# SwiGLU_1's opening in staircase order, its first two modulation columns on TensorE, and the mixer's first projection ahead of its norm

## The chip, the core and the metric

The kernel runs on one core of a Trainium2 chip. The metric is the device time of one execution in microseconds (us): the median of the timed runs. Engines are named as in the profile: PE is TensorE (matmuls), PEld its weight loads, DVE VectorE, ACT ScalarE, POOL GpSimd and SP SyncE, which issues most DMAs.

## The reference

One decoder layer of a batch of one: T = 256 tokens, model width D = 2048, feed-forward width FF = 5632, all in float32.

```
x = x + 1/2 * gate1 * SwiGLU_1(mod(norm(x)))          # shift 0, scale 1, gate 2 of nine adaLN vectors
x = x + gate2 * W_out [ FoX(heads 0..7) || GatedDeltaNet(heads 0..7) ](mod(norm(x)))   # shift 3, scale 4, gate 5
x = x + 1/2 * gate3 * SwiGLU_2(mod(norm(x)))          # shift 6, scale 7, gate 8
out = norm(x)

mod(norm(x)) = x * rsqrt(mean(x*x) + eps) * g * (1 + scale) + shift
swiglu(h)    = (silu(h @ wg) * (h @ wu)) @ wd
nine vectors = silu(c) @ ada_w + ada_b                # ada_w: 2048 x 18432, 144 columns of 128 outputs
```

The mixer has one input projection. It gives queries, keys and values of 8 forgetting-attention heads (FoX: softmax attention whose logits take a cumulated log forget gate) and of 8 gated-delta-net heads (a causal convolution of 4 taps, silu, L2 norm, and a recurrence over chunks of 64), besides small gates.

## The kernel before

**Layout.** Features lie on the 128 partitions, so x is 16 slices (`x[:, j]`, `KD` = 16) of 128 features x 256 tokens. All large products are exact to float32 by a split: an operand is a rounded high half plus a low remainder, and each 128x128 tile of a weight takes three matmuls, high x high, high x low and low x high (`three`, `mm`, `products`; matmuls into `pgu`, `pd`, `pp`).

**The weight stream.** `W` (class `Stream`) hands out weight tiles in the order in which the program asks for them. 8 tiles are a block of 512 KB, 674 blocks in all. `W.block(b)` issues the DMA to `wraw` on SP and the cast to the high half `whi` on ACT (L123); `W.next` adds the remainder `wlo` = `wraw` - `whi` on DVE (L135). FFN 1 takes blocks 0 to 263: 112 for the first 28 of 44 feed-forward slices of gate and up (`gate_up_first`), 56 for their down projection, 64 for gate and up of the other 16 slices, 32 for their down projection. The mixer starts at block 264.

**The adaLN columns.** Each of the 144 columns is 1 MB, and DVE reduces it against silu(c) in one instruction (L260, `adat` or `adaf`). `RATE` lists from which block on how many columns are handed out for each block (`W.side`). `ada_need` says that a column must be there before what follows. SwiGLU_1 needs 32 of them (shift 0 and scale 1, in turns by j) before its 16 slices of normalized input.

**The start.** ACT sums the squares of x and takes silu of c, which four one-row matmuls spread over the partitions (`pcs`, L658); PE turns x into features by 32 transposes (`px`, L679) and the reciprocal norm into a row (`nrow`, L709); DVE takes the first two columns in halves (`first_col`, L694). Warm-up matmuls on zeros (`zp`, L201) stand at two places (`N_WARM`).

**The first half of SwiGLU_1.** For slice j of the input, `modulate_one` makes `ht` on DVE (L368), the high half of `hs` on ACT, and the low half on DVE (L372 for odd j, L376 for even j). `gate_up_first` covers the inner dimension k in chunks 0 to 2, 2 to 8 and 8 to 16 (`CHUNKS`). In each chunk the 28 slices go in groups of 8, 8, 8 and 4; the first group goes k by k for the first 2, 5 and 5 values (`LEAD`), everything else slice by slice. Partial sums go to `acc`: 28 copies on ACT after the first chunk, 28 additions on DVE after the second, and the last chunk closes with silu and product.

**The norms.** A norm needs the sum of squares (`nsum`), its reciprocal root, and that as a row (`nrow`). Before the mixer, `modulate(1, 3, 4)` does all this, and then the first projection starts, slice by slice as `hs` is made (L769 to L771). For SwiGLU_2, the class `Early` does it another way: the first products are of x times the gain, ahead of the norm; the row then multiplies the result, and the shift is added through two more columns of the moving operand (`scaled`).

**The mixer.** Its steps are Python generators. Each `yield` states how much PE time should pass until its next part; the list `ORDER` says which heads come when. The keys' squared norms need a transposing matmul (`pkk`, L937) and an evacuation on ACT; `decays` is a run of logarithms and exponentials on ACT (L905). A FoX head has the places `plog` (logits), `ppt` (transposed weights, L1167), `pfo` (output), `pft` (transposed output, L1189).

**Order on an engine.** The program's order is not the order of issue: a list scheduler puts each engine's instructions in a fixed order when the kernel is built, and `tc.issue_after` and `tc.keep_in_program_order` bind it. At run time each engine goes through its own list in order.

Of the kernel before, what the change touches and what calls it, by code (L numbers as in the profile page):

```python
# [16 lines left out]
P = 128  # L17
D = 2048
# [5 lines left out]
CHUNKS = (0, 2, 8, 16)  # L24
LEAD = (2, 5, 5)
# [8 lines left out]
RATE = ((0, 0.5), (24, 0.34), (56, 0.45), (68, 0.06), (112, 0.5), (168, 0.38), (264, 0.0), (284, 0.26), (404, 0.0), (424, 0.125))  # L34
# [3 lines left out]
N_WARM = (10, 7)  # L38
# [3 lines left out]
LATER = 8  # L42
BEHIND = 2
# [47 lines left out]
class Stream:  # L91


    def __init__(self, nc, w, raw, hi, lo):
        self.nc, self.w, self.raw, self.hi, self.lo = nc, w, raw, hi, lo
        self.order = []
        self.more = None
        self.h = self.l = self.last = None
        self.owed, self.side, self.quiet = 0.0, lambda: None, False
        self.tc, self.hold, self.held = None, None, []  # L100
        self.first = []
        self.late, self.owing = False, []

    def settle(self, upto=N_TILES):

        while self.owing and self.owing[0][0] <= upto:
            self.owing.pop(0)[1]()

    def behind(self, later=True):
# [3 lines left out]
        return nullcontext() if self.hold is None else self.tc.issue_after(self.hold)  # L113

    def block(self, b):
# [7 lines left out]
        self.cast = self.nc.scalar.copy(self.h, r).ins  # L123
        return r, lo

    def next(self, mat, k, n, width=1):
        i = len(self.order)
        if i % WB == 0:
# [5 lines left out]
            with self.behind():  # L134
                lo_ = nc.vector.tensor_tensor(self.l, r, self.h.bitcast(F32), ALU.subtract)  # L135
            with self.tc.issue_after(lo_.ins):
                self.settle(b - BEHIND)
# [12 lines left out]
def layer_kernel(ctx: ExitStack, tc: tile.TileContext, xrow, c, adaw, cols, cst, w, out, order, dbg=None):  # L150
# [86 lines left out]
    def ada_col():  # L237
# [26 lines left out]
        if W.late:  # L264
            W.owing.append((len(W.order) // WB, total))
# [3 lines left out]
    def ada_need(m, j):  # L269
# [3 lines left out]
        W.settle()  # L273
# [81 lines left out]
    plain = hsf[:, : KD * HS].rearrange("p (k i) -> p k i", k=KD)[:, :, : 2 * T].rearrange("p k (q t) -> p k q t", q=2)  # L355

# [7 lines left out]
    def modulate_one(j, g1, sh, r, weave=True):  # L364

        t = pt("ht")
        hl, hh, tt = (run(j, LO), run(j, HI), turns(t)) if weave else (plain[:, j, LO], plain[:, j, HI], t)
        V.scalar_tensor_tensor(t, x[:, j], g1, r, ALU.mult, ALU.mult)  # L368
        if j % 2:
# [3 lines left out]
        else:  # L373
            with tc.issue_after(W.cast) if W.first else nullcontext():
                A.activation(hh, tt, AF.Identity, bias=sh)  # L375
# [9 lines left out]
    def modulate(which, m_sh, m_sc):  # L385
        ada_need(max(m_sh, m_sc), KD - 1)
        g1 = gains(which, m_sc, 0, KD)
        r = norm_row(norm_sums())
        hq["next"], hq["one"] = 0, lambda j: modulate_one(
            j, g1[:, j : j + 1], mod[:, m_sh * KD + j : m_sh * KD + j + 1], r, False)  # L390

    class Early:
# [3 lines left out]
        def __init__(self, which, m_sh, m_sc):  # L396
            self.which, self.m_sh, self.m_sc, self.row, self.rstd = which, m_sh, m_sc, None, None

        def y(self, j):
# [8 lines left out]
            A.activation(run(j, HI), turns(x[:, j]), AF.Copy, scale=g)  # L408
            V.scalar_tensor_tensor(run(j, LO), turns(x[:, j]), g, run(j, HI).bitcast(F32), ALU.mult, ALU.subtract)  # L409

        def step(self, k):
# [3 lines left out]
            if k == 4:  # L415
# [3 lines left out]
                    j, g1[:, j : j + 1], mod[:, self.m_sh * KD + j : self.m_sh * KD + j + 1], self.row)  # L419
# [8 lines left out]
        def scaled(self, dst, ps):  # L428
# [4 lines left out]
            V.tensor_tensor(dst, ps[:, :T], self.row, ALU.mult)  # L433
# [118 lines left out]
    def gate_up_first(fs, hp):  # L552
# [5 lines left out]
        groups = [fs[i : i + 8] for i in range(0, len(fs), 8)]  # L558
        chunks = list(zip(CHUNKS[:-1], CHUNKS[1:]))
# [17 lines left out]
        def evacuate(ps, f, ci):  # L577
            if ci == 0:
                acc[f] = hp.tile([P, 2 * T], F32, name="acc", tag="hid")
                A.copy(acc[f], ps)  # L580
            elif ci < len(chunks) - 1:
# [7 lines left out]
        for ci, (k0, k1) in enumerate(chunks):  # L589
            for gi, grp in enumerate(groups):  # L590
                if gi == 0 and LEAD[ci]:
                    pb = {f: bank() for f in grp}
                    ks = k0 + LEAD[ci]
                    for k in range(k0, ks):
                        ada_need(0, k)
                        for f in grp:
                            for s in range(2):
                                three(pb[f], f, s, k, k0, k1)
                    for f in grp:
                        for k in range(ks, k1):  # L600
                            ada_need(0, k)
                            for s in range(2):
                                three(pb[f], f, s, k, k0, k1)
                        evacuate(pb[f], f, ci)
                else:
                    for f in grp:
                        pf = bank()
                        for k in range(k0, k1):
                            ada_need(0, k)
                            for s in range(2):  # L610
                                three(pf, f, s, k, k0, k1)
                        evacuate(pf, f, ci)
        return hids

    def ffn(which, m_gt, early=None):
        fs = list(range(NF))
        with tc.tile_pool(name=f"hid{which}", bufs=PARTS[which][1] + HIDX) as hp, \
                tc.tile_pool(name=f"more{which}", bufs=1) as more:
            W.more = more if MORE else None
            for half in range(2):  # L620
# [7 lines left out]
                def after(j):  # L628
                    residual(pds.pop(j), j, m_gt, True)
                    if half == 1:  # L630
                        sumsq_add(j)
                        if which == 1:
# [22 lines left out]
    pcs = []  # L655
    for q in range(4):
        pcs.append(psn(q + 1, "pcs"))
        PE.matmul(pcs[q], one[:1], crow[:, q * 512 : (q + 1) * 512], start=True, stop=True)  # L658

# [6 lines left out]
    for kind, i in (("x", 0), ("x", 1), ("c", 0), ("c", 1), ("x", 2), ("x", 3), ("c", 2), ("c", 3)):  # L666
        with nullcontext() if hold is None else tc.issue_after(hold):
            if kind == "c":
                hold = cond(i)
            else:  # L670
# [4 lines left out]
    def features(i):  # L675
        px = psn(i, "px")
# [6 lines left out]
    for i in range(4):  # L683
        features(i)
# [760 lines left out]
```

## Time and profile before

| | |
|---|---|
| median of 3 runs | 1943.49 us (1943.44 to 1944.72) |
| profiled execution, own time | 1943.79 us |
| its span | 1941.9 us, from the first to the last instruction |
| mean granted TensorE clock | 0.992 |
| PE busy | 1903.0 us, 98% of the span |
| PEld, DVE, ACT, POOL busy | 1777.2, 1554.0, 1041.2, 56.8 us |
| first matmul into `pgu` | 22.52 us |
| FFN 1, mixer, FFN 2 with the last norm | to about 741 us, to about 1238 us, to the end |

Shares are of the whole span. PE busy at 98% says little about where time can be had: a stage in which PE waits, or in which its clock is granted at half, shows only in views of that stage. Busy PE time also counts matmuls that run at half the clock.

### The profile page before, as it was taken

The numbers are of one execution on the slowest core, as the hardware profiler recorded it, in microseconds if no ns is written. First come the engines' busy times: TensorE is split into PE (matmuls) and PEld (weight loads), VectorE is DVE, ScalarE is ACT, GpSimd is POOL, SyncE is SP. The second block draws the span as 40 slices with busy tenths as digits, with TensorE's granted clock in tenths as the row PEclk, the third lists the DMA queues.
The fourth block names the chain that finished last, engine by engine and source line by source line (L and its number), as shares of the span: only waits on it lengthen the run. The fifth ranks groups of instructions, "written<-read, shape, count | busy, mean of one in ns | idle before, by whom it ended". The sixth has DMA issues, their size and how long they took to land. (4 is left out here: it accounts for less than half of the span.)

```text
span 1941.9 us, 33701 instructions
## 1 busy us (share of the span) xinstructions
PE 1903.0 (98%) x13087; PEld 1777.2 (92%) x13087; DVE 1554.0 (80%) x2415; ACT 1041.2 (54%) x1647; POOL 56.8 (3%) x55
## 2 busy tenths in 40 slices
PE   8999999999999999999999999999999999999998
PEld 6999999998999988889989998999999999999997
DVE  6999978989989997779987989976777665666654
ACT  6544555433455446858657655665554445555553
POOL 0000000000000030000000001100000000000011
PEclk8999999999999999999999999999999999999999
DMA  9989867999999975586667568667767665565663
GB/s 371 359 308 358 305 224 258 400 369 376 356 358 339 361 302 212 212 314 220 214 242 257 201 218 303 208 258 252 245 253 257 244 225 200 201 200 202 202 200 120
DMA packets 129490, 519.58 MB, mean 268 GB/s; under 512 B 18217, under 2 KB 21545, under 8 KB 111153
## 3 DMA queue, kind: packets, MB, share of 16 engines
q1 hardware_dynamic: 129330, 517.42, 72.9%
q8 instruction: 103, 1.69, 0.3%
q14 instruction: 57, 0.47, 0.1%
HBM read 512.89 MB, written 4.47 MB: 266 GB/s over the span
## 5 line engine op out<-in xcount | busy, mean ns | idle before, releaser
L135 DVE TENSOR_TENSOR wlo<-wraw,whi 128x1024 fp32r<-128x1024 f32 x674 | 822.3, 1226 | 268.3 <-ACT whi L123 267.3
L123 ACT CAST whi<-wraw 128x1024 fp32r<-128x1024 f32 x674 | 700.6, 1047 | 515.1 <-PE pd L485 166.5
L485 PE MATMUL pd<-hid,whi 128*128 128x512 f32 x1408 | 461.8, 382 | 0.0
L486 PE MATMUL pd<-hid,wlo 128*128 128x256 f32 x1408 | 384.6, 273 | 2.6 <-DVE wlo L135 2.6
L260 DVE CUSTOM_DVE_ANT_0 adat<-adat,cs,colt 128x2048 f32<-128x2048 f32 x140 | 329.2, 2351 | 6.5 <-DMA adat<-in_ada_dram 6.5
L481 PE MATMUL pg<-hs,whi 128*128 128x512 f32 x912 | 302.2, 382 | 0.5 <-DVE shc L432 0.5
L481 PE MATMUL pu<-hs,whi 128*128 128x512 f32 x912 | 302.2, 382 | 0.0
L485 PEld LDWEIGHTS pd<-hid,whi 128*128 128x128 f32 x1408 | 266.0, 189 | 36.9
L486 PEld LDWEIGHTS pd<-hid,wlo 128*128 128x128 f32 x1408 | 270.3, 192 | 5.4 <-DVE wlo L135 5.3
L567 PE MATMUL pgu<-hs,whi 128*128 128x256 f32 x896 | 245.8, 277 | 5.9 <-ACT hs L371 5.9
L482 PE MATMUL pu<-hs,wlo 128*128 128x256 f32 x912 | 249.2, 273 | 0.0
L482 PE MATMUL pg<-hs,wlo 128*128 128x256 f32 x912 | 248.9, 273 | 0.0
L569 PE MATMUL pgu<-hs,wlo 128*128 128x256 f32 x896 | 245.1, 278 | 2.4 <-DVE wlo L135 2.4
L568 PE MATMUL pgu<-hs,whi 128*128 128x256 f32 x896 | 246.5, 277 | 0.0
L481 PEld LDWEIGHTS pg<-hs,whi 128*128 128x128 f32 x912 | 172.4, 189 | 24.8 <-ACT shc L431 0.7
L481 PEld LDWEIGHTS pu<-hs,whi 128*128 128x128 f32 x912 | 172.4, 189 | 23.6
L769 PE MATMUL pp<-hs,whi 128*128 128x256 f32 x656 | 188.9, 289 | 1.6 <-ACT hs L375 1.6
L770 PE MATMUL pp<-hs,whi 128*128 128x256 f32 x656 | 182.9, 279 | 0.0
L771 PE MATMUL pp<-hs,wlo 128*128 128x256 f32 x656 | 182.7, 278 | 0.0
L567 PEld LDWEIGHTS pgu<-hs,whi 128*128 128x128 f32 x896 | 172.9, 194 | 6.7 <-ACT hs L371 6.3
L482 PEld LDWEIGHTS pu<-hs,wlo 128*128 128x128 f32 x912 | 175.0, 192 | 1.0 <-DVE wlo L135 0.9
L482 PEld LDWEIGHTS pg<-hs,wlo 128*128 128x128 f32 x912 | 175.1, 192 | 0.4
(337 smaller groups left out, 2593.8 us busy)
## 6 DMA issues: line engine op xcount, KB each, us to landing
wraw<-in_w_dram SPq DMA_DIRECT2D x674, 512.0 KB, 4.4
adat<-in_ada_dram SPq DMA_DIRECT2D x140, 1024.0 KB, 7.2
xr<-in_xr_dram SPq DMA_DIRECT2D x4, 512.0 KB, 5.3
adaf<-in_ada_dram SPq DMA_DIRECT2D x4, 512.0 KB, 8.5
adaf<-in_ada_dram SPq DMA_DIRECT2D x2, 1024.0 KB, 12.3
xd<-x SPq DMA_DIRECT2D x4, 512.0 KB, 7.0
rw<-rowd SPq DMA_DIRECT2D x16, 128.0 KB, 4.3
x<-xd SPq DMA_DIRECT2D x4, 512.0 KB, 5.8
```

What stands on the lines that cost most here:

```text
L123: self.cast = self.nc.scalar.copy(self.h, r).ins
L135: lo_ = nc.vector.tensor_tensor(self.l, r, self.h.bitcast(F32), ALU.subtract)
L260: V.tensor_tensor_reduce(t, t, cs, 1.0, L("adab", q, 1), ALU.mult, ALU.add, mod[:, q : q + 1])
L481: PE.matmul(ps, wt[0], both, start=(k == 0), stop=False)
L482: PE.matmul(ps[:, T:], wt[1], part(k, HI), start=False, stop=(k == KD - 1))
L485: PE.matmul(ps, wt[0], act.rearrange("p q (a b) -> p q b a", a=2), start=first, stop=False)
L486: PE.matmul(ps[:, :T], wt[1], woven(act[:, 0]), start=False, stop=last)
L567: PE.matmul(o, wh, part(k, HI), start=first and s == 0, stop=False, skip_group_check=skip)
L568: PE.matmul(o, wh, part(k, LO), start=False, stop=False, skip_group_check=skip)
L569: PE.matmul(o, wl, part(k, HI), start=False, stop=last, skip_group_check=skip)
L769: PE.matmul(pp[i][:, :T], wh, hh, start=(k == 0), stop=False)
L770: PE.matmul(pp[i][:, :T], wh, hl, start=False, stop=False)
```

## The change

1. **Staircase.** In `gate_up_first` the table `PIECES` (group, first k, k by k up to, last k) takes the place of `CHUNKS` and `LEAD`. The four groups take turns at the low k, so that a slice of the input is used by many matmuls before the next is asked for. Evacuations are put off in a list `owed`. There are 28 copies on ACT as before; of additions on DVE there are 32 in the place of 28. The sums of the columns are finished behind the next block's `wlo` from the start (`W.late`).
2. **First two columns on PE.** silu(c) is also made as columns (`pct`: 16 one-column matmuls; `csk`), and the first two adaLN columns are 16 matmuls each of one column (`pcol`, L717 of the changed kernel), whose weights the host has packed for it. `px` uses three PSUM buffers of one pool. Half of the `pcs` matmuls come later. Block 0 is cast and subtracted in two halves. Warm-up matmuls: 10, 2 and 2 in the place of 10 and 7.
3. **First projection of the mixer ahead of its norm.** `Early` serves here too (`norm1`); `modulate` and the layout `plain` go. The gates and three key heads are scaled by the row and shifted afterwards.
4. **Residuals later.** In the feed-forward parts the residual of one output slice is placed at step 18 (at most the last but one) of the next slice, before at step 8.
5. **RATE.** The pace of the columns is retuned.
6. **Spacing.** FoX steps ask for 1.5, 4.5, 1.5 and 6.5 in the place of 1, 3, 1 and 5; `decays` for 3 in the place of 1.

The diff, cut:

```diff
-CHUNKS = (0, 2, 8, 16)
-LEAD = (2, 5, 5)
+PIECES = (
+    (0, 0, 1, 1), (1, 0, 1, 1), (2, 0, 2, 2), (3, 0, 3, 3), (0, 1, 4, 4), (1, 1, 6, 6), (3, 3, 7, 7),
+    (2, 2, 11, 11), (3, 7, 12, 12), (0, 4, 11, 16), (1, 6, 6, 16), (2, 11, 11, 16), (3, 12, 12, 16),
+)
-RATE = ((0, 0.5), (24, 0.34), (56, 0.45), (68, 0.06), (112, 0.5), (168, 0.38), (264, 0.0), (284, 0.26), (404, 0.0), (424, 0.125))
+RATE = ((0, 0.5), (12, 0.45), (68, 0.06), (112, 0.5), (168, 0.42), (232, 0.24), (264, 0.0), (288, 0.27), (404, 0.0), (424, 0.125))
-N_WARM = (10, 7)
+N_WARM = (10, 2, 2)
-LATER = 8
+LATER = (18, 8)
...
+        owed = []
+        for g, k0, ks, k1 in PIECES:
+            grp = fs[8 * g : 8 * g + 8]
+            pb = {}
...
+            for k in range(k0, ks):
+                for f in grp:
+                    both(f, k)
+            for f in grp:
+                for k in range(max(k0, ks), k1):
+                    both(f, k)
+                owed.append(lambda f=f, ps=pb[f], k0=k0, k1=k1: evacuate(ps, f, k0, k1))
+                while ks < k1 and len(owed) > 1:
+                    owed.pop(0)()
...
+    pct = psf("pct")
+    for k in range(KD):
+        PE.matmul(pct[:, k : k + 1], crow[:, k * P : (k + 1) * P], one[:1, :1], start=True, stop=True)
...
+    def first_col(i):
+        m, j = ada_seq[i]
+        q = m * KD + j
+        for k in range(KD):
+            PE.matmul(pcol[:, i : i + 1], first_ada[i][:, k * P : (k + 1) * P], csk[:, k : k + 1], start=(k == 0),
+                      stop=(k == KD - 1), skip_group_check=True)
+        return V.tensor_tensor(mod[:, q : q + 1], pcol[:, i : i + 1], L("adab", q, 1), ALU.add)
...
-        modulate(1, 3, 4)
...
-        first = project([("gt", 0)] + [("qkv", NH + h) for h in range(3)])
+        W.lag = 2
+        first = project([("gt", 0)] + [("qkv", NH + h) for h in range(3)], norm1)
...
-                        if j and q == LATER:
+                        if j and q == min(LATER[0], len(part) - 2):
                             after(j - 1)
...
-            yield 3.0
+            yield 4.5
             ppt = psf("ppt")
```

PE's own order at the start, from the warm-up matmuls to the first product of SwiGLU_1 (`pgu`). Before:

```order
L201 MATMUL zp<-zw 128x512
L658 MATMUL pcs<-crow,one 128x512 x4
L679 MATMUL px<-colt,xr 128x128 x24
L709 MATMUL nrow<-colt,frb 128x128 x2
L679 MATMUL px<-colt,xr 128x128 x8
L201 LDWEIGHTS zw
```

and in the changed kernel:

```order
L676 MATMUL pcs<-crow,one 128x512 x2
L682 MATMUL pct<-one,crow 128x1 x16
L706 MATMUL px<-colt,xr 128x128 x12
L717 MATMUL pcol<-csk,adaf_118 128x1 x3
L706 MATMUL px<-colt,xr 128x128 x8
L717 MATMUL pcol<-csk,adaf_118 128x1 x5
L706 MATMUL px<-colt,xr 128x128 x5
L717 MATMUL pcol<-csk,adaf_118 128x1 x8
L733 MATMUL nrow<-colt,frb 128x128 x2
L706 MATMUL px<-colt,xr 128x128 x7
L676 MATMUL pcs<-crow,one 128x512 x2
```

Behind these stand two warm-up matmuls, 16 of L717 for the second column, two more warm-up matmuls and the first `pgu`. So 48 one-column matmuls have come into PE's queue ahead of it, and 3 of 17 warm-up matmuls have gone.

DVE's own order at the same place, from the first low half of `hs` on (`adaf` is a column prefetched at the start, `adat` one that streams). Before:

```order
L376 SCALAR_TENSOR_TENSOR hs<-ht,mod,hs 128x2x128
L135 TENSOR_TENSOR wlo<-wraw,whi 128x1024 x2
L260 ISA adaf_120,mod<-adaf_120,cs,colt 128x2048
L260 ISA mod 128x1
L260 ISA adaf_121,mod<-adaf_121,cs,colt 128x2048
L260 ISA mod 128x1
L382 SCALAR_TENSOR_TENSOR g_320<-mod,colt 128x1
L135 TENSOR_TENSOR wlo<-wraw,whi 128x1024
L368 SCALAR_TENSOR_TENSOR ht<-x,g_320,nrow 128x256
L135 TENSOR_TENSOR wlo<-wraw,whi 128x1024
L372 TENSOR_TENSOR hs<-ht,hs 128x2x128
```

and in the changed kernel:

```order
L393 SCALAR_TENSOR_TENSOR hs<-ht,mod,hs 128x2x128
L146 TENSOR_TENSOR wlo<-wraw,whi 128x512 x2
L146 TENSOR_TENSOR wlo<-wraw,whi 128x1024 x2
L272 ISA adaf_120,mod<-adaf_120,cs,colt 128x2048
L272 ISA mod 128x1
L146 TENSOR_TENSOR wlo<-wraw,whi 128x1024 x2
L272 ISA adaf_121,mod<-adaf_121,cs,colt 128x2048
L272 ISA mod 128x1
L399 SCALAR_TENSOR_TENSOR g_443<-mod,colt 128x1
L146 TENSOR_TENSOR wlo<-wraw,whi 128x1024
L380 SCALAR_TENSOR_TENSOR ht<-x,g_443,nrow 128x256
L393 SCALAR_TENSOR_TENSOR hs<-ht,mod,hs 128x2x128
```

The second slice of the input now comes behind six subtractions of blocks (the first in two halves) where it came behind four, and three of them, before two, stand ahead of the first column (`adaf_120`).

PE's own order where FFN 1 ends and the mixer begins. Before:

```order
L485 MATMUL pd<-hid,whi 128x512
L486 MATMUL pd<-hid,wlo 128x256
L323 MATMUL nsum<-colt,sqacc 128x2 x2
L323 MATMUL nsum<-colt,sq 128x2 x2
L342 MATMUL nrow<-colt,rb 128x128 x2
L769 MATMUL pp<-hs,whi 128x256 x4
```

and in the changed kernel, where `nrow` comes up:

```order
L435 MATMUL pp<-hs,whi 128x258
L436 MATMUL pp<-hs,whi 128x256
L437 MATMUL pp<-hs,wlo 128x258
L356 MATMUL nrow<-colt,rb 128x128 x2
L435 MATMUL pp<-hs,whi 128x258
L436 MATMUL pp<-hs,whi 128x256
L437 MATMUL pp<-hs,wlo 128x258
```

The products `pp` of the mixer now stand on both sides of `nrow` (and of `nsum`), where they all stood behind it.

More of the change, by code (lines that the diff above doesn't have):

```diff
@@ L122, in block @@
         self.h = hi.tile([P, WB * P], F32R, name="whi")
-        self.cast = self.nc.scalar.copy(self.h, r).ins
+        with nullcontext() if b != 1 else self.tc.issue_after(self.lead):
+            one, *more = self.pieces(b)
+            h = self.h
+            self.cast = self.nc.scalar.copy(h[:, one], r[:, one]).ins
+            self.rest += [lambda q=q: self.nc.scalar.copy(h[:, q], r[:, q]).ins for q in more]
         return r, lo
@@ L264, in ada_col @@
         if W.late:
[L265 removed]
+            W.owing.append((len(W.order) // WB, i, total))
         else:
@@ L557, in gate_up_first @@
         W.hold, W.held = None, [ada_done[0, 0]().ins]
-        groups = [fs[i : i + 8] for i in range(0, len(fs), 8)]
-        chunks = list(zip(CHUNKS[:-1], CHUNKS[1:]))
+        W.late = True
         acc, hids = {}, []
@@ L711, in layer_kernel @@
     hold = A.copy(first_row, pr[:, :T]).ins
-    for i in range(4, KD // 2):
+    for i in (6, 7):
         features(i)
+    spread(2, pss)
+    spread(3, pss)
     with tc.issue_after(nr.ins):
         warm_up(N_WARM[1])
-    W.first.append(W.block(0))
-    first_col(0, 1)
-    first_col(1, 0)
-    first_col(1, 1)
+    first_col(1)
+    warm_up(N_WARM[2])
+    with tc.issue_after(hold):
+        W.first.append(W.block(0))
+    W.rest += [lambda q=q: cond(q) for q in (2, 3)]
     ada_st["i"] = 2
```

186 lines of the change are left out of this document (96 added, 90 removed).

## The prediction

> **What bounds the kernel now.** I read the page first, then the busy times by stage, then the list of what PE waits for, then PE's own timeline at the start. The page:
>
> ```profile
> span 1941.9 us, 33701 instructions
> PE 1903.0 (98%) x13087; PEld 1777.2 (92%) x13087; DVE 1554.0 (80%) x2415; ACT 1041.2 (54%) x1647; POOL 56.8 (3%) x55
> ```
>
> PE sets the end, so only places where PE waits, or where its clock is halved, can give time. Those show by stage (start and end: length, then busy us of PE, PEld, DVE, ACT and POOL with their instructions, PEclk, DMA share, GB/s):
>
> ```profile
> 22.40:125.00 102.60, 94.29 (x793) 92.67 (x792) 94.66 (x106) 54.56 (x75) 0.00 (x0) 0.96 0.90 346
> 125.00:335.00 210.00, 210.00 (x1883) 210.00 (x1883) 187.73 (x262) 104.67 (x142) 0.00 (x0) 1.00 0.79 291
> 741.20:753.60 12.40, 8.06 (x43) 7.70 (x41) 10.95 (x26) 5.55 (x11) 1.74 (x7) 0.72 0.36 128
> ```
>
> The middle row is the yardstick: 1883 matmuls in 210 us without a gap, 0.1115 us each. By it the 793 of the first row need 88.4 us of 102.6, so the opening of SwiGLU_1 loses **14.2 us**; the 43 of the last row, the step from FFN 1 to the mixer, need 4.8 of 12.4 and lose **7.6 us**. What PE waits for (total, times, longest):
>
> ```profile
> PE pgu L567 <- ACT hs L371: 5.9, 2, 3.6
> PE nrow L709 <- DVE frb L708: 3.2, 1, 3.2
> PE pkk L937 <- ACT kk L941: 2.7, 1, 2.7
> PE pd L486 <- DVE wlo L135: 2.6, 9, 0.6
> PE pgu L569 <- DVE wlo L135: 2.4, 4, 1.5
> PE pp L769 <- ACT hs L375: 1.6, 1, 1.6
> PE nrow L342 <- DVE rb L341: 1.5, 1, 1.5
> PE pft L1189 <- issue: 1.4, 1, 1.4
> PE ppt L1167 <- ACT x L1162: 1.3, 2, 1.1
> PE nsum L323 <- ACT sq L309: 1.3, 1, 1.3
> ```
>
> The opening waits for input slices (5.9 us) and remainders of blocks (2.4 us); the rest of its 14.2 us is half clock behind the waits:
>
> ```profile
> 6.07:9.49 3.42, 3.42 (x9) 1.19 (x8) 0.00 (x0) 3.21 (x8) 0.00 (x0) 1.00 1.03 391
> 9.49:12.90 3.41, 3.41 (x17) 3.41 (x17) 1.53 (x4) 2.94 (x8) 0.00 (x0) 0.50 1.03 376
> 12.90:16.31 3.41, 1.06 (x10) 0.81 (x8) 3.31 (x12) 1.28 (x3) 0.00 (x0) 1.00 1.01 412
> 26.55:29.97 3.42, 1.98 (x18) 1.79 (x17) 3.42 (x6) 0.00 (x0) 0.00 (x0) 1.00 1.02 416
> 29.97:33.38 3.41, 1.28 (x9) 1.11 (x10) 3.41 (x5) 0.94 (x2) 0.00 (x0) 1.00 0.99 413
> 33.38:36.80 3.42, 3.42 (x19) 3.42 (x18) 3.19 (x5) 2.61 (x4) 0.00 (x0) 0.50 1.04 434
> ```
>
> The clock is granted for stretches of 3.41 us by what PE did in the stretch before: after 1.28 us of work comes 0.50, after 1.98 us the clock stays. Each dip costs about 1.7 us.
>
> **1. The first two columns on PE.** PE at the start:
>
> ```profile
> 5.61 3.91 PE L658 MATMUL pcs<-crow,one 1*128 1x512 f32 x8
> 9.45 4.51 PE L679 MATMUL px<-colt,xr 128*128 128x128 f32 x24
> 17.16 1.22 PE L709 MATMUL nrow<-colt,frb 128*128 128x128 f32 x4 [3.21 <-DVE frb L708]
> 18.18 1.92 PE L679 MATMUL px<-colt,xr 128*128 128x128 f32 x8
> 19.89 3.19 PE L201 MATMUL zp<-zw 128*128 128x512 bf16 x7
> 22.52 0.77 PE L567 MATMUL pgu<-hs,whi 128*128 128x256 f32 x1
> ```
>
> PE had 3.2 idle us here. Now 48 one-column matmuls are queued on it, the last 16 of them directly ahead of the first `pgu`: its input needs the shift that they give, and DVE, ACT and PE all stand behind it. There is no such matmul in the trace; the nearest rows are eight columns wide:
>
> ```profile
> 789.70 0.39 PE L849 MATMUL pcum<-x,cstt 128*128 128x8 f32 x2
> 789.95 0.37 PE L850 MATMUL pcum<-x,cstt 128*128 128x8 f32 x2
> ```
>
> Two records each, started 0.25 us apart, 0.22 in runs of them; I take 0.222 at full clock and twice 0.213 = 0.426 at half (the 8 `px` of the row at 18.18 take 0.213 each there at the queue's pace, 1.71 us to the next row). The Trainium skill ("TensorE: Matmul & The Clock Gate", Back-to-back issue gap) gives very narrow matmuls an issue floor of about 25 ns; by that 32 of them would cost 0.8 us and the start would come some 6 us sooner than below. The 0.25 us of these rows speaks against it.
>
> The sum along PE's queue: half of `pcs` ends at 5.61 + 3.91/2 = 7.6. The 16 `pct` have one-row weights, like `pcs`, whose 8 loads take 1.19 us: 32 records of 0.16 end at 12.8. 12 `px` and 3 of the first column at half clock: 12 x 0.213 + 3 x 0.426, to 16.6. If those count as work for the clock, all later is at full: 20 `px` and 4 `nrow` records x 0.111, 13 x 0.222, 4 `pcs` records x 0.22, two warm-ups at 0.22, 16 x 0.222, together 10.4, to 27.0; 0.8 for handing the three `px` buffers over, 1.2 for DVE's addition, ACT's high half and the handover. So `pgu` starts at 29.0 in the place of 22.5: **+6.5**. At full clock from 9.49 on it would be 26.3 (+3.8).
>
> **2. The staircase.** DVE's prices in the opening:
>
> ```profile
> L135 DVE TENSOR_TENSOR wlo<-wraw,whi 128x1024 fp32r<-128x1024 f32 x64 | 77.3, 1222 | 6.7 <-ACT whi L123 6.5
> L260 DVE CUSTOM_DVE_ANT_0 adat<-adat,cs,colt 128x2048 f32<-128x2048 f32 x26 | 61.0, 2347 | 0.4 <-DMA adat<-in_ada_dram 0.4
> L582 DVE TENSOR_TENSOR acc<-pgu,acc 128x512 f32<-128x512 f32 x28 | 19.1, 688 | 0.6 <-PE pgu L569 0.4
> L368 DVE SCALAR_TENSOR_TENSOR ht<-x,g,nrow 128x256 f32<-128x256 f32 x14 | 6.8, 485 | 0.4
> L376 DVE SCALAR_TENSOR_TENSOR hs<-ht,mod,hs 128x256 fp32r<-128x256 f32 x8 | 3.9, 482 | 2.8 <-ACT hs L375 2.8
> ```
>
> A block is 24 matmuls, 2.68 us of PE, and 1.22 us of DVE. A slice of input is two columns, `ht` and `hs`: 2 x 2.35 + 0.97 = 5.66 us of DVE. Before, slice 1 is asked for after two k by k passes' first, 5.3 us of PE: DVE needs 5.66 + 2 x 1.22 = 8.1, late by 2.8 (with a longest wait of 3.6 in the list). Slice 7 is asked for at 64 us: 7 x 5.66 + 24 x 1.22 = 68.9, late again. In the new order PE asks for slices 1, 2, 3, 7 and 12 at 16, 26.7, 40, 109 and 181 us after the first `pgu`. DVE needs 12.9, 23.5, 35.2, 89.4 (and some `acc`) and about 172 with 22 us of `acc`. All are in time, by 3 us and more. Nor is the DMA queue late: at the 416 GB/s of the row at 26.55 a block (0.52 MB) takes 1.3 us and a column (1.05 MB) 2.5; up to slice 7 that is 41 blocks and 16 columns, 93 us, where PE asks at 29 + 109; and SP's list only changes one column's place with a block's. On ACT the casts of blocks and the 28 copies stay as many as they were; the second half of block 0's cast and half of silu(c) now stand behind the first `hs`, and only the third column, three remainders later on DVE, needs them. What stays: columns ahead of remainders in DVE's one queue, since DVE has 165 us to do in 160 of PE around block 60; running the sum along its order leaves the worst remainder 1.6 to 2.9 us late, with one dip behind it and small change, 5.2 us. **-9.0** (from -5, if ACT's casts, 6.5 us of idle DVE, come as late as before, to -12).
>
> RATE then puts more columns into the rest of FFN 1, where DVE had 0.985, 0.906 and 0.919 of PE's time by the same sums and now has 1.003, 0.948 and 0.931; `pd L486` already waits 2.6 us for remainders there. Residuals at step 18 only move 32 short DVE instructions. **+1.0** (0 to 3).
>
> **3. The projection ahead of the norm.** 64 tiles of three matmuls, two of them 258 wide, are 21.6 us of PE ahead of which only the last slice's product with its gain must be ready. The sum of squares (1.3), the row (1.5) and `hs` (1.6) are covered, and the dip goes with them. What is late next: PE's next projection takes a bank that DVE evacuates first, and in DVE's order this stands behind 16 modulations and 4 remainders, at about 24 us, where PE is there at 22.8. That leaves 1.4, the last residual and the row 0.5, gates and their sums 0.5, and 0.7 for a chance of a dip: 3.1 of 7.6. **-4.5** (-1 to -7).
>
> **4. `decays` and FoX.** The wait of `pkk` comes from ACT, on which exponentials with two table loads stand ahead of the key's evacuation:
>
> ```profile
> L905 ACT ACTIVATE Ln<-Ln,colS 128x128 f32<-128x128 f32 x8 | 2.4, 387 | 0.0
> L905 ACT ACT_TABLE_LOAD x1 | 1.3, 1283 | 0.0
> ```
>
> In ACT's new order they stand behind the second key. 2.7 of wait and about 1.9 of half clock are 4.6; I leave 1.6: **-3.0** (0 to -4.7). In FoX `ppt` (1.3) and `pft` (1.4) get more matmuls ahead of them, 5.4 us for 3.8 and 9.55 for 9.1; one head, the sixth, has its `pft` drawn nearer, 3.6 us for 7.1, against a chain of 3.9: -2.7 + 0.8, **-1.9** (+0.5 to -3.5).
>
> **Sum.** +6.5 - 9.0 + 1.0 - 4.5 - 3.0 - 1.9 = -10.9. The profiled execution's own time is 1943.8 (span 1941.9 and 1.9 around it), 0.3 over the median: 1943.8 - 10.9 - 0.3 = **1932.6**.
>
> **The rivals.** *A: one-column matmuls do not count for the clock.* The window 6.07 to 9.49 is full of one-row matmuls, and yet 0.50 follows; the new start has 48 narrow ones. For it: if they count like `pcs`, the clock stays at half to the first `pgu`. Against it: 17 transposes in a window do bring full clock, and so would the new order's `px`, if enough of them fall into one window. Then 12 `px` and 3 columns are followed by 20 `px` and 4 `nrow` x 0.213, 29 x 0.426, `pcs` 2.0, warm-ups 1.8: 16.6 + 21.3 = 37.9, `pgu` at 39, and 2 us more until the clock comes back: +18.5, and 1943.8 - 0.3 + 18.5 - 17.4 = 1944.6. It decides by the price of a record at half clock, for which loads bound from above:
>
> ```profile
> L770 PEld LDWEIGHTS pp<-hs,whi 128*128 128x128 f32 x9 | 3.0, 333 | 0.0
> L770 PEld LDWEIGHTS pp<-hs,whi 128*128 128x128 f32 x43 | 8.3, 192 | 0.0
> ```
>
> A load takes 0.333 at half and 0.192 at full, of which 0.111 shows when loads overlap matmuls; 0.213 and 0.333 are the bounds. From 0.257 on 64 records of the two columns bring it past +3.9, and at 0.28 it is **1949**, slower. The Trainium skill (the same page, PE-mode transpose) says that transposes do not count as busy PE either, which would make this rival sure. The windows at 9.49 (transposes) and 12.90 (clock 1.00) do not agree.
>
> *B: the opening stays bound by DVE and ACT.* The 14.2 us are kept, only shifted: casts late, `acc` in a bunch. For it: DVE is busy 94.7 of 102.6 us there, and idle 6.5 waiting for casts; against it: the needs above. 1932.6 + 9 = **1942**.
>
> *C: full clock at the start.* +3.8 for +6.5: **1930**.
>
> **How the numbers follow.** The forecast 0.47, A 0.28, B 0.14, C 0.11. About 0.2% (3.9 us) is what a measurement can tell. Forecast and C are faster, and a little of B: 0.60. B mostly, and A at low prices: 0.17. A from 0.257 on: 0.23. The range: below, the sum of the better ends (C, -12, -7, -4.7) would be near 1922; above, A at 0.28 with a little more, 1950.
>
> **What would show it.** The first `pgu` near 29 (26 by C, 39 by A), and the clock row from 16.3 on. Between the first `pgu` and 100 us later, 5 us lost in the place of 14.2, with waits for remainders and none for `hs`. No wait at `nsum` or `nrow` of the mixer's norm; one of 1 to 3 us at the first product of the third projection. No `pkk` wait of over 2 us. I am wrong if `pgu` waits for `hs` as before, or if the start eats more than 12 us.

## The result, and the profile after

The changed kernel takes 1970.87 us (1967.67 to 1971.66, 4 runs) against 1943.47 of the kernel before: **1.0142 times as long, interval 1.0129 to 1.0155**. The forecast was 1932.6, with 1922 to 1950 as its range. The profiled execution's own time is 1970.26. (One of the ten executions of t_fix below took 2174.3 us at a mean granted clock of 0.844; the times of t_fix are given without it.) The page of the changed kernel, and three stretches of it: the opening, the second gate and up of FFN 1, and from the second down projection to the first product behind the early projection of the mixer (start and end, length, busy us of PE, PEld, DVE, ACT and POOL, PEclk, DMA share, GB/s):

```profile
span 1967.6 us, 34033 instructions
PE 1924.2 (98%) x13180; PEld 1796.0 (91%) x13180; DVE 1563.8 (79%) x2455; ACT 1046.4 (53%) x1667; POOL 55.5 (3%) x55
```

```profile
39.40:142.00 102.60, 93.85 (x782) 93.04 (x782) 91.62 (x105) 54.41 (x75) 0.00 (x0) 0.93 0.85 324
509.00:687.00 178.00, 172.45 (x1028) 154.33 (x1027) 159.71 (x186) 84.02 (x127) 0.00 (x0) 1.00 0.93 345
742.00:797.00 55.00, 51.99 (x380) 49.14 (x378) 52.23 (x95) 34.54 (x61) 8.18 (x13) 1.00 0.65 220
```

The opening starts at 39.4 us, and by the prediction's yardstick (0.1115 us a matmul) its first 102.6 us hold 87.2 us of work: 15.4 lost, where it was 14.2. The middle row is a stage that the prediction hardly looked at. What PE waits for, the longest rows:

```profile
PE pgu L580 <- DVE acc L595: 5.3, 6, 2.3
PE pgu L580 <- ACT acc L593: 5.0, 1, 5.0
PE pg L496 <- DVE wlo L146: 4.3, 7, 0.9
PE po L500 <- DVE wlo L146: 2.7, 2, 1.8
PE pd L500 <- DVE wlo L146: 2.4, 6, 0.5
PE pp L800 <- DVE shc L443: 2.3, 1, 2.3
PE pp L800 <- ACT whi L132: 2.1, 1, 2.1
```

No row names `nsum` or `nrow` any more, and `hs` stands in one of 0.3 us alone, in FFN 2: those waits of before are gone, as forecast. In their place stand banks that wait for partial sums (`acc`, 10.3 us), and remainders.

The stages, each from the last matmul of the one ahead of it to its own last (the start: to the first `pgu`; the norm: to the first `pkk`; the mixer: to the first output product), with the loss against the usual spacing of the same matmuls in brackets, in us:

| stage | before | changed | start undone | projection alone |
|---|---|---|---|---|
| start | 22.5 | 39.4 | 21.7 | 21.3 |
| opening of SwiGLU_1 | 314.2 (16.0) | 318.7 (20.4) | 317.1 (18.8) | 314.6 (16.3) |
| first down | 150.0 (2.6) | 150.7 (3.3) | 150.7 (3.3) | 150.0 (2.6) |
| second gate and up | 168.8 (0.4) | 177.8 (9.3) | 177.8 (9.3) | 170.4 (2.0) |
| second down | 85.6 (1.4) | 83.8 (-0.4) | 83.8 (-0.4) | 83.9 (-0.3) |
| norm to `pkk` | 57.8 (8.6) | 57.4 (6.1) | 57.6 (6.3) | 54.5 (5.2) |
| mixer, its output | 435.7 | 432.2 | 435.0 | 435.0 |
| FFN 2 | 699.7 | 700.0 | 699.7 | 699.9 |

The two columns on the right are experiments s_dve and b_early below. The change loses its time in three rows: 16.9 at the start, 4.5 in the opening, 9.0 in the second gate and up. Gains are 1.8 in the second down and 3.6 from there on.

At the start, PE's timeline (start us, length, line, tiles, records) and the clock windows:

```profile
12.77 2.82 PE L706 MATMUL px<-colt,xr 128*128 128x128 f32 x12
15.38 1.28 PE L717 MATMUL pcol<-csk,adaf 128*128 128x1 f32 x6
16.52 1.95 PE L706 MATMUL px<-colt,xr 128*128 128x128 f32 x8
...
21.35 3.41 PE L717 MATMUL pcol<-csk,adaf 128*128 128x1 f32 x16
...
27.25 3.78 PE L676 MATMUL pcs<-crow,one 1*128 1x512 f32 x4
...
31.79 6.83 PE L717 MATMUL pcol<-csk,adaf 128*128 128x1 f32 x32
...
39.42 0.79 PE L580 MATMUL pgu<-hs,whi 128*128 128x256 f32 x2
```

```profile
12.90:16.31 3.41, 3.41 (x18) 3.41 (x18) 0.83 (x6) 3.38 (x8) 0.00 (x0) 0.50 1.00 398
16.31:19.73 3.42, 3.42 (x18) 3.42 (x18) 1.44 (x8) 1.58 (x3) 0.00 (x0) 0.50 1.03 431
33.38:36.80 3.42, 3.42 (x18) 3.42 (x18) 0.00 (x0) 0.00 (x0) 0.00 (x0) 0.50 0.00 0
36.80:40.21 3.41, 3.41 (x14) 2.55 (x15) 0.97 (x3) 1.37 (x3) 0.00 (x0) 0.50 0.00 0
```

32 records in 6.83 us are 0.213 each, the half-clock price that the prediction had for its rival A. The window from 33.38 is filled with one-column matmuls, PE is busy in all of it, and 0.50 follows all the same.

Then the opening's first wait. ACT and DVE in the changed kernel around it (DVE's `adaf` at 48.64 is the fourth column):

```profile
51.03 2.05 ACT L593 COPY acc<-pgu 128x512 f32<-128x512 f32 x4 [3.44 <-DVE mod L272]
```

```profile
46.37 2.36 DVE L146 TENSOR_TENSOR wlo<-wraw,whi 128x1024 fp32r<-128x1024 f32 x2
48.64 2.35 DVE L272 CUSTOM_DVE_ANT_0 adaf<-adaf,cs,colt 128x2048 f32<-128x2048 f32 x1
```

ACT's copy of a finished bank has nothing to do with a column, and yet it starts when that column is done. The program puts the partial sums into memory in which the prefetched columns lay; f_acc below shows that this is the wait. Eight banks are full after one slice of input, and PE stands for 5.0 us.

### The profile page after: what moved, and what is told of

Its sections match the earlier page's. It is cut to its first block, busy times and chain, and to the rows that moved or that the text cites. A ratio compares the mean times of both kernels' runs of the same rounds, so it can differ in the third digit from the quotient of the medians.

```text
span 1967.6 us, 34033 instructions
## 1 busy us (share of the span) xinstructions
PE 1924.2 (98%) x13180; PEld 1796.0 (91%) x13180; DVE 1563.8 (79%) x2455; ACT 1046.4 (53%) x1667; POOL 55.5 (3%) x55
## 4 chain that ended last, share of the span: by engine, by line
PE 72%; DVE 10%; issue 4%; ACT 2%; DMA 1%; SPq 0%; DVEq 0%; ACTq 0%
PE pd L499 14%; PE pu L495 9%; PE pg L495 9%; PE pd L500 7%; PE pu L496 5%; PE pg L496 4%; DVE wlo L146 4%; PE pgu L580 3%; PE pgu L582 3%; PE pgu L581 3%; DVE adat L272 2%; PE pp L800 2%; PE pp L801 2%; PE pp L802 2%; PE po L499 1%
## 5 line engine op out<-in xcount | busy, mean ns | idle before, releaser
L146 DVE TENSOR_TENSOR wlo<-wraw,whi 128x1024 fp32r<-128x1024 f32 (+1 forms) x675 | 822.2, 1221 | 279.5 <-ACT whi L132 277.2
L132 ACT CAST whi<-wraw 128x1024 fp32r<-128x1024 f32 (+1 forms) x674 | 701.0, 1045 | 539.7 <-PE pd L499 148.9
L580 PE MATMUL pgu<-hs,whi 128*128 128x256 f32 x896 | 249.7, 279 | 10.5 <-DVE acc L595 5.3
L581 PE MATMUL pgu<-hs,whi 128*128 128x256 f32 x896 | 248.5, 278 | 0.0
L580 PEld LDWEIGHTS pgu<-hs,whi 128*128 128x128 f32 x896 | 174.5, 195 | 12.8 <-issue 6.2
L800 PE MATMUL pp<-hs,whi 128*128 128x256 f32 x592 | 170.9, 289 | 4.4 <-DVE shc L443 2.3
L581 PEld LDWEIGHTS pgu<-hs,whi 128*128 128x128 f32 x896 | 174.3, 195 | 0.0
L582 PEld LDWEIGHTS pgu<-hs,wlo 128*128 128x128 f32 x896 | 173.8, 194 | 0.5 <-DVE wlo L146 0.5
```

The source lines that it names most:

```text
L132: self.cast = self.nc.scalar.copy(h[:, one], r[:, one]).ins
L146: lo_ = nc.vector.tensor_tensor(self.l[:, q], r[:, q], self.h[:, q].bitcast(F32), ALU.subtract)
L580: PE.matmul(o, wh, part(k, HI), start=first and s == 0, stop=False, skip_group_check=skip)
L581: PE.matmul(o, wh, part(k, LO), start=False, stop=False, skip_group_check=skip)
L582: PE.matmul(o, wl, part(k, HI), start=False, stop=last, skip_group_check=skip)
L800: PE.matmul(pp[i][:, :T], wh, hh, start=(k == 0), stop=False)
```

## The experiments

**The start.** Undone in s_dve, alone in b_start, with wide matmuls in w_wide.

s_dve, the changed kernel with

```diff
-N_WARM = (10, 2, 2)
+N_WARM = (10, 7)
...
-    first_col(0)
...
+    first_col(0, 0)
```

(the first two columns in halves on DVE again; `pcs` and block 0 are as before, too)

> The changed kernel with its start undone: the first two columns by DVE, the spreading matmuls, the warm-up matmuls and block 0 as before; all else as changed. Theory 1 (the start costs its 16.9 us by itself, half clock and 48 one-column matmuls; the rest of the loss lies elsewhere): first pgu near 22.5 us, time 1952 (1950 to 1954), and the opening still loses 15 us or more. Rival (the late start also starves what follows, since casts and transfers stand still for 14 us): 1946 or less, with an opening that loses under 10 us.

1950.5 us (1949.6 to 1952.8), ratio 1.0046 (1.0031 to 1.0061): theory 1. `pgu` starts at 21.7, and the opening still loses 18.8. The start is worth 20.3 us by the medians, 18.7 by the ratios; the rival, which had it starve the opening too, falls.

b_start, the kernel before with

```diff
+    for k in range(KD):
+        PE.matmul(pcol[:, i : i + 1], first_ada[i][:, k * P : (k + 1) * P], csk[:, k : k + 1], ...)
```

> The kernel before with only the changed start. Theory 1: first pgu near 39.4 us, 1961 (1959 to 1964). Rival (the start only costs together with the staircase, and the chunks of before make up for part of it, since two columns fewer are asked of DVE): 1955 or less.

1956.9 us, ratio 1.0080 (1.0055 to 1.0106), but the four runs lie at 1952.5, 1953.8, 1959.9 and 1963.4, wider than any other kernel here (at most 7.9 us, in 21 executions of the kernel before). The profiled one took 1953.8:

```profile
18.76 1.84 PE L715 MATMUL pcol<-csk,adaf 128*128 128x1 f32 x16
...
25.45 6.82 PE L715 MATMUL pcol<-csk,adaf 128*128 128x1 f32 x32 [0.22 <-issue]
...
33.08 0.80 PE L582 MATMUL pgu<-hs,whi 128*128 128x256 f32 x2
```

```profile
16.31:19.73 3.42, 3.42 (x34) 3.42 (x33) 1.37 (x8) 2.00 (x4) 0.00 (x0) 1.00 1.04 436
19.73:23.14 3.41, 3.41 (x22) 2.73 (x23) 0.80 (x3) 1.92 (x4) 0.00 (x0) 0.95 0.99 408
23.14:26.55 3.41, 3.19 (x9) 1.56 (x9) 0.00 (x0) 0.00 (x0) 0.00 (x0) 0.50 1.04 432
```

The same list of PE, 0.1 us earlier, got the full clock for most of the transposes and of the first column, and lost it again about where the one-row matmuls (`pcs`) stand, so that the second column ran at half clock all the same. So the forecast's mixed case does occur, but not its "all later is at full". Neither theory had that. Why the executions differ so much is not shown: one was traced, and the mean granted clocks of the four (0.990, 0.990, 0.987 and 0.994, in the order above) do not follow their times.

w_wide, the changed kernel with

```diff
-            PE.matmul(pcol[:, i : i + 1], first_ada[i][:, k * P : (k + 1) * P], csk[:, k : k + 1], ...)
+            PE.matmul(pcol[:, i * P : (i + 1) * P], first_ada[i][:, k * P : (k + 1) * P], csk[:, k : k + 1].to_broadcast([P, P]), ...)
```

> The changed kernel with the 32 matmuls of the first two columns taking a moving operand of 128 equal columns in the place of one. Theory 1 (one-column matmuls do not count as work for the clock, and at half clock are paid by their weights' load, so that 128 columns cost no more): granted clock 1.00 by 23 us, first pgu at 28 to 32, time 1960 to 1964. Rival (the clock goes by something else, or wider matmuls cost more): first pgu at 39 or later, 1970 or more.

1959.3 us (1959.0 to 1960.5), ratio 1.0091 (1.0076 to 1.0106): theory 1, a little below its time. 128 times the columns made the kernel faster, by 11.6 us by the medians and 9.9 by the ratios:

```profile
17.52 3.55 PE L717 MATMUL pcol<-csk,adaf 128*128 128x128 f32 x30
...
25.10 3.73 PE L717 MATMUL pcol<-csk,adaf 128*128 128x128 f32 x32
...
29.64 0.49 PE L580 MATMUL pgu<-hs,whi 128*128 128x256 f32 x2 [0.38 <-ACT hs L387]
```

```profile
16.31:19.73 3.42, 3.42 (x27) 3.42 (x26) 1.40 (x8) 1.53 (x3) 0.00 (x0) 0.81 1.02 429
19.73:23.14 3.41, 3.41 (x29) 3.14 (x29) 0.80 (x3) 1.58 (x4) 0.00 (x0) 1.00 1.03 422
```

32 records take 3.73 us for 6.83, with the clock at 1.00 from the second row on. `pgu` at 29.6 is near the 29.0 that the forecast had.

**The opening.** f_acc is s_dve with

```diff
-N_FIRST = 4
+N_FIRST = 2
```

> The changed kernel with its start undone (1950.5 us), and N_FIRST 2 in the place of 4, so that the third and fourth column are loaded into the streaming buffers and no longer into memory that the first partial sums take over. Theory 1 (ACT's first copy of a partial sum waits for the fourth column's reduction, since both lie in the same memory, and PE's banks wait for the copies): the wait of 5.8 us at 27 us goes, and the half clock behind it, time 1943.5 (1942 to 1946). Rival (the copies then wait for something else, or the columns come later from two buffers): 1949 or more.

1950.9 us (1949.6 to 1952.7): no gain; theory 1 is wrong in its number, and the time is the rival's. What PE waits for in the opening, in s_dve and then in f_acc:

```profile
PE pgu L580 <- DVE acc L595: 5.7, 7, 2.3
PE pgu L580 <- ACT acc L593: 5.6, 1, 5.6
PE pgu L582 <- DVE wlo L146: 0.3, 1, 0.3
```

```profile
PE pgu L580 <- DVE acc L595: 4.7, 3, 2.2
PE pgu L582 <- DVE wlo L146: 4.0, 6, 1.9
```

The copies' wait is gone, as the mechanism has it; but the remainders are late by 4.0 us in its place, and the loss only falls from 18.8 to 17.8 us. PE, no longer held up at 27 us, catches up with DVE.

b_stair is the kernel before with the staircase alone (`PIECES` for `CHUNKS` and `LEAD`, the early pace, and this line, which stands in the change's `gate_up_first`):

```diff
+        W.late = True
```

> The kernel before with the staircase alone (with its early pace of columns, and totals of columns finished behind the next block's remainder, in all of FFN 1). Theory 1 (the staircase takes away the waits for input slices and pays as much for banks that wait for copies and additions; totals behind the remainders cost 3 us in the second gate and up): opening 317 us with a loss of 18 to 19, second gate and up with a loss near 3, time 1949 (1947 to 1951). Rival (totals cost nothing there, the 3 us seen so far belong to the later residuals): loss there 0.4, 1946 or less.

1955.7 us (1955.1 to 1958.0), ratio 1.0072 (1.0057 to 1.0087), slower than theory 1 had it. The opening loses 19.2, the second gate and up 3.3, as expected. The second down loses 4.6 for 1.4, the first down 4.1 for 2.6: there, too, totals are finished late. The mixer's output loses 7.3 for 3.6, which the lateness does not explain, since the kernel before has `W.late` in the mixer as well; that part stays open. (The edit also carries the change's layout of `hs` in the mixer, and its rule that a needed column finishes only the columns ahead of it.)

p_lo asked whether DVE's queue alone is the bound. The kernel before with

```diff
-                lo_ = nc.vector.tensor_tensor(self.l, r, ...)
+                lo_ = (nc.gpsimd if 8 <= b < 264 and b % 6 == 2 else nc.vector).tensor_tensor(self.l, r, ...)
```

> The kernel before with the remainder of every sixth block of FFN 1 subtracted on POOL, from block 8 on. Theory 1 (DVE's queue is the bound of FFN 1's opening): loss there 9 to 12 us for 16, time 1938 (1936 to 1941). Rival (POOL takes 5 us for one and delays the block, or shares a port with DVE): 1946 or more.

1968.1 us (1965.0 to 1968.4), ratio 1.0130 (1.0115 to 1.0145): the rival, though at half its price for one:

```profile
L135 POOL TENSOR_TENSOR wlo<-wraw,whi 128x1024 fp32r<-128x1024 f32 x43 | 120.9, 2812 | 574.5 <-ACT whi L123 458.2 <-DVE mod L260 48.4 <-DVE wlo L135 30.0
```

```profile
L260 DVE CUSTOM_DVE_ANT_0 adat<-adat,cs,colt 128x2048 f32<-128x2048 f32 x140 | 347.4, 2481 | 8.1 <-DMA adat<-in_ada_dram 8.1
```

A remainder takes 2.81 us there for 1.22 on DVE, and a column on DVE 2.48 us on the mean for 2.35 otherwise. The opening is no faster (loss 16.6), and the first down loses 13.3 us for 2.6. So the run leaves open whether DVE's queue alone bounds the opening: the subtractions came back later from POOL, and DVE's own columns took longer beside them.

**The later stages of FFN 1.** r_rate, the changed kernel with

```diff
-(168, 0.42), (232, 0.24), (264, 0.0), (288, 0.27)
+(168, 0.38), (264, 0.0), (284, 0.26)
```

> The changed kernel with the pace of columns of before from block 168 on (0.38 up to block 264, 0.26 from 284). Theory 1 (0.42 columns a block are more than DVE and the casts behind it carry in the second half of gate and up): the waits for remainders there go from some 9 us to 1, time 1963 (1961 to 1965). Rival (these waits come from the residuals' new place or from totals finished behind the next block): 1969 to 1971.

1972.6 us (1971.1 to 1974.2): theory 1 falls in this form. The second gate and up does go from 9.3 to 3.3, but the second down from -0.4 to 7.1: the loss moved with the columns.

e_off, s_dve with the mixer's projection behind its norm and that same pace:

```diff
-        first = project([...], norm1)
+        modulate(1, 3, 4, runs)
+        first = project([...])
```

> The changed kernel with its start undone (1950.5 us), and with the mixer's first projection again behind its norm and the pace of before from block 168 on. Theory 1 (the products of x and gain put 10 us of DVE work into the last stage of FFN 1, and the pace that makes room for it overloads the stage before): the loss in the second gate and up goes from 9.3 us to 1 or less, that in the step to the mixer from 6.1 to 8.6, time 1945.5 (1944 to 1947). Rival (the losses in FFN 1 come from the residuals at step 18 and totals behind the next block): 1951 or more, slower by what the norm then costs.

1950.6 us (1948.9 to 1954.1): no gain. The second gate and up still loses 3.3 and the second down 4.5, at the pace at which the kernel before loses 0.4 and 1.4. Something else than pace and projection was costing there. fe is e_off with

```diff
-N_FIRST = 4
+N_FIRST = 2
```

> Both f_acc and e_off in one: what is left of the change is the staircase, the later residuals and the spacing. Theory 1, by sums: 1950.5 - 7 - 5 = 1938.5, faster than the kernel before. Rival (the gains are not additive, since DVE's queue is the bound of the whole of FFN 1): 1943 or more.

1951.2 us (1949.0 to 1953.2): the rival.

b_early, the kernel before with the projection ahead of the norm and the changed pace from block 168 on, but no staircase and no `W.late`:

```diff
+                        if which == 0:
+                            norm1.y(j)
...
-        first = project([...])
+        first = project([...], norm1)
```

> The kernel before with the mixer's first projection ahead of its norm alone, with the changed pace of columns from block 168 on. Theory 1 (the pace of 0.42 overloads DVE and ACT in the second gate and up): loss there 9 us for 0.4, last down projection 1.7 better, the norm 2.4 better, time 1948 (1946 to 1950). Rival (the loss there comes from totals that wait behind remainders, which this kernel does not have): 1941 or less.

**1939.0 us (1938.5 to 1942.7, 10 runs), ratio 0.9987 (0.9977 to 0.9996): faster than both kernels**, and the rival right: at 0.42 columns a block the stage loses 2.0 us, not 9.3. So pace by itself is not the cause, and the lateness is left: before, the program issues a column's total when the column is handed out; with `W.late` the total waits in `owing` until the next block's remainder stands on DVE. t_off is s_dve with

```diff
         while owed:
             owed.pop(0)()
+        W.settle(10 ** 9)
+        W.late = False
         return hids
```

> The changed kernel with its start undone (1950.5 us), and with the totals of columns finished where they were before (not behind the next block's remainder) from the end of the opening on; the staircase itself, the pace, the projection ahead of the norm stay. Theory 2 (this lateness, which came with the staircase, and not the pace by itself, makes the second gate and up lose 9.3 us): loss there 2 to 3 us, time 1943 (1941 to 1945). Rival (the pace loses it by itself with this order of columns): 1949 or more.

1941.9 us (1940.4 to 1944.5, 10 runs), ratio 1.0002 (0.9993 to 1.0011): theory 2. Loss in the second gate and up 1.9. t_on is b_early with

```diff
+        W.late = True
         return hids
```

> The kernel before with the mixer's first projection ahead of its norm and the changed pace (1939.0 us), and now with totals finished behind the next block's remainder from the end of the opening on. Theory 2: the second gate and up loses 9 us where it lost 2, time 1946.5 (1945 to 1948). Rival (it costs only together with the staircase): 1938 to 1941.

1949.0 us (1948.3 to 1949.5), ratio 1.0033 (1.0020 to 1.0046): theory 2: 10.0 us by the medians, 8.9 by the ratios to the kernel before, for one line. In the profiled executions 6.5 us of it lie in the second gate and up (176.9 for 170.4), 1.1 and 0.9 in the two down projections. Who waits in the same 170 us of both, nearly all of the second gate and up (486 to 656 us), in b_early and then in t_on:

```profile
DVE wlo L144 <- ACT whi L130: 4.8, 13, 0.5
...
ACT tg L527 <- DVE tg L505: 7.1, 13, 0.9
```

```profile
DVE wlo L144 <- ACT whi L130: 9.8, 9, 1.4
...
ACT tg L527 <- DVE tg L505: 20.1, 13, 3.1
...
PE pu L494 <- DVE wlo L144: 3.7, 7, 0.9
PE pg L494 <- DVE wlo L144: 1.0, 2, 0.5
```

Moved by one place, the 2.35 us column stands in front of `tg` on DVE; ACT's silu waits for `tg` (20.1 us for 7.1), the cast of the next block is queued behind that silu, DVE's next remainder waits for the cast (9.8 for 4.8), and PE for the remainder. DVE is not full (same stretch, b_early and then t_on):

```profile
486.00:656.00 170.00, 169.73 (x1023) 153.87 (x1022) 158.36 (x186) 83.06 (x124) 0.00 (x0) 1.00 0.94 360
486.00:656.00 170.00, 165.09 (x989) 148.69 (x989) 151.66 (x177) 81.17 (x120) 0.00 (x0) 1.00 0.93 353
```

In b_early DVE is 0.93 busy, 158.4 of 170 us, and PE is busy in 169.7; in t_on it is 0.89 busy, 151.7 us, and PE is busy in 165.1. So it is the order in the loop over the two queues that costs here, and not the amount of work.

**Spacing and residuals.** y_off is s_dve with the old yields:

> The changed kernel with its start undone (1950.5 us), and the spacing of the FoX steps and of decays as before. The prediction's step (spacing saves 1.9 us in FoX and, with ACT's order, 3.0 at pkk): 1955. Theory 1 (the waits only change places, since the stage's loss was 20.5 us before and 20.6 after): 1949 to 1952.

1952.5 us (1950.6 to 1953.3), against 1950.5 of s_dve; the ratios' intervals (1.0033 to 1.0063 and 1.0031 to 1.0061) lie on each other, so no effect is shown, and 4.9 us is out. By stages the old spacing makes norm and mixer 3.4 us shorter and the output 4.1 longer; a part of that is work on the other side of a bound (18 matmuls at the first `pkk`). The wait at `pkk` is 0.5 us with either spacing. b_later is the kernel before with the residuals at step 18:

> The kernel before with the later residuals alone. Theory 1 (residuals at the end of a short product let DVE's work meet the next residual, 3 us in the second down projection of FFN 1): 1946 (1945 to 1947.5). Rival (nothing, as the prediction has it): 1942 to 1944.

1944.3 us (1941.7 to 1946.4, 10 runs), ratio 1.0009 (0.9999 to 1.0018): within what can be told from nothing; the second down loses 1.4 as before.

**Do the causes add up?** t_fix is t_off with the change of N_FIRST, t_wide is w_wide with all of this (`W.late` goes off at the end of the opening):

```diff
-N_FIRST = 4
+N_FIRST = 2
...
+        W.settle(10 ** 9)
+        W.late = False
```

> As t_off, and with the third and fourth column out of the memory of the first partial sums. Theory 2: what is left of the staircase loses 17 to 18 us in the opening against 16.3 of the kernel before with the projection alone, time 1942 (1940 to 1944), no faster than that one (1939.0). Rival (freed of both costs, the staircase gains): 1937 or less.

> The whole change with three repairs: moving operands of 128 equal columns for the first two columns, the third and fourth column out of the memory of the first partial sums, totals as before after the opening. Theory 2: 1970.9 - 11.5 - 1 - 7.5 = 1951 (1948 to 1953), first pgu at 28 to 31. Rival (the later start moves the opening's columns against its blocks, and the repairs do not add up): 1955 or more.

t_fix: 1941.4 us (1939.2 to 1943.8, 9 runs), ratio 0.9997 (0.9987 to 1.0006): theory 2. t_wide: 1948.9 us (1947.7 to 1952.6), ratio 1.0037 (1.0022 to 1.0051), first `pgu` at 32.7, 2 us later than expected. Start and lateness hold the loss: with both undone (t_off) the kernel takes as long as the one before. What is left of the staircase, free of both its costs, loses 16.7 us in the opening against 16.3 of b_early: it gains nothing. PE waits there 5.1 us for additions to `acc` and 4.9 for remainders, where in b_early it waits 6.4 for `hs` and 2.4 for remainders. Whether the staircase would gain at another pace of columns in the opening, no run tried.

## Why the prediction was wrong, point by point

The result lies 38.3 us above the forecast. By the table of stages the start holds 10.4 of them, the staircase 13.5, the pace in FFN 1 6.9, and all from the norm on 5.8; the rest is between profiled executions and medians.

**The start (+6.5).** Wrong in the choice between its own cases. The sum along PE's queue held: rival A had `pgu` at 39, it came at 39.4, with 0.213 a record. The failed step is "if those count as work for the clock, all later is at full". A window of 12 transposes with one-column matmuls among them did not raise the clock, and one full of one-column matmuls did not either; in b_start, where the clock did come up at 16 us, it fell again at 23, ahead of the second column. The sign that the prediction named for itself, a start that eats more than 12 us, came true with 16.9. The Trainium skill ("TensorE: Matmul & The Clock Gate", PE-mode transpose), by which transposes do not count as busy PE, fits the windows of the changed kernel; b_start's 1.00 in the window from 16.3 does not agree, so the rule is too strong for these runs.

**The staircase (-9.0).** The failed step is the sum of DVE's needs. It was right for what it counted, the slices of input: no `hs` wait is left. It left out what the order does to the banks. One slice of input for eight slices of output fills all eight banks in 5.4 us, and they come free only through a copy on ACT (held up by a column's memory, 5.0 us) or an addition on DVE, which stands behind remainders and columns (5.3). I had read `acc` as a number of additions, not as what PE waits for. Rival B, with its 14.2 us kept in another place, was the better picture; measured, the opening's loss rises by 2.8 (s_dve) instead of falling by 9, and with the memory freed and the totals back in their place (t_fix) it is still 16.7.

**Pace in FFN 1 (+1.0, at most 3).** Mis-sized at 8 to 9. I priced the pace by DVE's share of PE's time (0.948 for the second gate and up) and gave `W.late` no price at all, though the order showed totals changing place. The runs put the cost on that line: 9 to 10 us when it is added alone (t_on), 8.6 saved when it is taken away (t_off), most of it in the second gate and up. The pace alone costs 1.6 in that stage and gives 1.6 back in the next.

**The projection ahead of the norm (-4.5).** Right. The norm's stage is 3.3 shorter in b_early, with a wait of 2.7 us at the first product behind the early projection, of the kind and size that was named; the whole kernel, with the new pace, is 3.7 us faster by the medians, 2.5 by the ratio. In the changed kernel the stage's loss falls as well, from 8.6 to 6.1, and is outweighed.

**`decays` and FoX (-4.9).** No gain is shown, and the failed step is to add the 3.0 at `pkk` to the gain of the early projection, since either takes the same wait away. With the projection behind its norm the old spacing has waits of 1.2 to 3.8 us at `pkk` (2.7 in the kernel before), the new spacing none (e_off, fe). With the projection ahead of the norm the wait is 0.5 under the old spacing (b_early, y_off) and 0.5 under the new (s_dve; 1.4 in the changed kernel). For FoX y_off shows no loss either.

**Residuals (0).** Right, by b_later.

## What to carry to other kernels

Before giving a lightly used engine small work, ask whether that work keeps its clock up, and not only whether the engine was idle: 48 narrow matmuls cost more than the 3.2 idle us that they were to fill, and with 32 of them widened the start cost 7.9 us more than on DVE, where it had cost 17.7. When an order is changed so that inputs come in time, follow the buffers as well, PSUM banks and memory that is used twice, since what no longer waits for its input will wait for its output. And read a change of place in a queue as a change of its own: reductions moved behind one subtraction each cost some 9 us in all with the same work on every engine, through a loop over two engines neither of which was full.

## What the runs showed of the hardware that was not expected

One PE list, started 0.1 us apart in two kernels, met the full clock in one (`pgu` at 33.1) and not in the other (39.4), and b_start's executions differ by 11 us (1952.5 to 1963.4). At full clock a matmul with 128 moving columns cost no more here than one with a single column: 0.117 us a record (w_wide, 3.73 us for 32) and 0.115 (b_start, 1.84 us for 16); at half clock the narrow one took 0.213. Beside subtractions on POOL, DVE's reduction of a column took 2.48 us on the mean in the place of 2.35.
